# The two meta rows of w_out: scaled sums on VectorE in place of matmuls on TensorE, in a one-core hybrid decoder layer

## The chip, the core and the metric

The kernel runs on one core of a Trainium2 chip. A core has a matrix engine, TensorE (PE in the profile; PEld is its weight load), and three engines that work on 128 partitions: VectorE (DVE), ScalarE (ACT) and GpSimd (POOL). DMA transfers are started from queues; here nearly all loads and stores stand in the queue of SyncE (SP), one after the other. Each engine works through its own queue in the order in which the program was built, and waits by semaphore for what the others have to deliver.

The metric is the device time of one execution, in microseconds (us). Before the change it was 1255.82, the median of three runs (1255.19 to 1255.9).

## The reference, cut to what matters

One layer with 1024 tokens of width 1024, in front of which 16 meta tokens are put. Two branches, attention and a convolution, are merged by gates to `mixed`, which goes through `w_out`; the FFN behind it is convolved over three tokens.

```python
y_attn = a @ w_attn_proj
y_conv = c @ w_conv_proj
mixed = jax.nn.sigmoid(g_attn) * y_attn + jax.nn.sigmoid(g_conv) * y_conv
h = layer_norm(DEEPNORM_ALPHA * h + mixed @ w_out, ln1_g, ln1_b)
up = causal_dwconv(h @ ffn_w_up, ffn_dw, ffn_dw_b)
...
return h[:, N_META:]
```

The meta tokens' rows are dropped at the end. But the causal convolution with three taps reads two tokens back, so the last two meta rows of `h` behind `w_out` are needed for the first two real tokens. These two rows are what the change is about: `mixed[2 rows, 1024] @ w_out[1024, 1024]`, the residual and the norm.

## The kernel before

The kernel works in fp32. A product of two fp32 operands is made on TensorE from three matmuls in the type fp32r: each operand is split into a high part (a cast, line 267, on ScalarE) and a low part (the difference, line 270, on VectorE or GpSimd), and high x high, high x low and low x high are added in PSUM (`product`, lines 296, 300 and 301).

The stage of the projections (loop over `m` from line 1080) computes `mixed` in eight tiles of 128 channels. For each `m` it makes four groups of columns `g`, each with a product of the attention branch (PSUM tag `mm`, three buffers) and one of the convolution branch (tag `t`, two buffers). VectorE reads both from PSUM and multiplies by the gates (lines 1099 and 1100), adds (1101), ScalarE writes the high part (1108), and VectorE the low part (1109). In group 0 the first two columns are the two meta tokens; they go into the small tile `pair`, high parts in columns 0 and 1, low parts in 2 and 3 (lines 1103 and 1104).

`w_out` is loaded in eight blocks `k` of 128 rows. Blocks 0 to 3 go to free parts of the buffer FA ("early", line 1125, each placed in SP's queue behind the last gate load of tile m = k), blocks 4 and 5 to FA and OB, blocks 6 and 7 to the two rotating buffers `wr`. `prep_wo` splits them. The low parts of blocks 4 to 7 are formed on GpSimd.

The output stage (`out_rows`, line 1230) takes 128 tokens at a time, in the order 3, then -1 (the two meta rows), 7, 2, 6, 0, 4, 1, 5. For a tile it makes two halves of 512 columns, 24 matmuls each. VectorE evacuates a half and adds the residual (line 1253), collects its statistics (1254), aggregates them (241), ScalarE makes the root (246), and VectorE refines it (247 to 249) and normalises the row (1277). The next tile but one half, `turn` transposes it on TensorE (1287) and ScalarE writes the result (1300). For the two meta rows the kernel before uses 16 matmuls per half: for each block `k` one with the four columns of `pair` against the high part of `w_out` (line 1264), and one with the two high columns against the low part (1265). The sum has four partitions; ScalarE copies it (1266), and partitions 2 and 3 are brought to 0 and 1 by a DMA through SP (line 1271) so that VectorE can add them (1272).

The order on each engine is not that of the text. A scheduler places the instructions by priority (`rank`) and by its own estimate of when they are ready; `after` adds an edge of order. The built program is then fixed.

Of the kernel before, what the change touches and what calls it, by code (L numbers as in the profile page):

```python
# [23 lines left out]
F = mybir.dt.float32  # L24
R = mybir.dt.float32r
AF = mybir.ActivationFunctionType
OP = mybir.AluOpType
AX = mybir.AxisListType

P = 128  # L30
D = 1024
KC = D // P
# [31 lines left out]
RK_CLN, RK_OSPLIT, RK_Z, RK_CONV, RK_PROJ = 38000, 39000, 40000, 60000, 70000  # L64
# [35 lines left out]
def tile_hybrid_layer(  # L100
# [3 lines left out]
    nc = tc.nc  # L104
# [5 lines left out]
    def load(o, i):  # L110
        return nc.sync.dma_start(out=o, in_=i)
# [5 lines left out]
    def f32(ap):  # L117
        return ap.bitcast(F)

    def after(ins, first):  # L120

        tc.add_manual_dep(ins.ins, first.ins.name, mybir.DependencyInfo(
            mybir.DependencyClass.NoSync, mybir.DependencyReason.SCHED_ONLY), reason="order of work")

    @contextmanager
    def rank(p):

        saved = tc.cur_priority
        tc.cur_priority = p
        yield  # L130
        tc.cur_priority = saved


    const = ctx.enter_context(tc.tile_pool(name="const", bufs=1, side="left"))
# [6 lines left out]
    FA = arena.tile([P, 6144], F, name="FA")  # L141
# [23 lines left out]
    start = ExitStack()  # L165
# [100 lines left out]
    def split(raw, hi, lo, quick=False, behind=None):  # L266
        ins = nc.scalar.copy(hi, raw)  # L267
        if behind is not None:
            after(ins, behind)
        return (nc.vector if quick else nc.gpsimd).tensor_tensor(lo, raw, f32(hi), OP.subtract)  # L270
# [747 lines left out]
    for g in range(3):  # L1018
# [5 lines left out]
    rx_p = ctx.enter_context(tc.tile_pool(name="rx", bufs=1, side="right", reuse_waits="tile"))  # L1024
    RX = rx_p.tile([P, 2112], R, name="RX")
    wo_stack = ExitStack()
    RW = wo_stack.enter_context(tc.tile_pool(name="rw", bufs=1, side="right", reuse_waits="tile")).tile(
        [P, 2048], R, name="RW")
    RT = OB[:, 0:2048]


# [19 lines left out]
    def prep_wo(k, raw=None, behind=None):  # L1051
        if k < 4:
            hi, lo = OA[:, k * 2048:k * 2048 + 1024], OA[:, k * 2048 + 1024:k * 2048 + 2048]
        elif k < 6:
            hi, lo = ((RX, RW)[k - 4][:, x:x + 1024] for x in (0, 1024))
        else:
            hi, lo = (wsp_p.tile([P, D], R, name=n, tag=n) for n in ("whi", "wlo"))
        if raw is None:
            raw = wraw([P, D])
            load(raw, w_out_v[k])  # L1060
        split(raw, hi, lo, k < 4, behind)
        wo[k] = (hi, lo)

    pair = const.tile([P, KC, 4], R, name="pair")
    const.tile([P, 16], F, name="pad_e")
    g_next = [0]

    GS = [(FA, i * 516) for i in range(4)]
# [11 lines left out]
    for m in range(KC):  # L1080
        hi, lo = weights([P, KC, P], lambda raw: load(raw, w_ab[m]))

        def branch(i, g, tag, bufs):
            a, b = PG[g]
            ps = pat.tile([P, 512], F, name="ps_p", tag=tag, bufs=bufs)
            rhs = (oo, conv)[i]
            product(ps[:, :b - a], [(hi[:, 4 * i + k], lo[:, 4 * i + k], rhs(k, 0, a, b), rhs(k, 1, a, b))
                                    for k in range(4)])
            return ps[:, :b - a]

        def merge(g, psa, psb):
            a, b = PG[g]
            n = b - a
            with rank(RK_EVAC):
                t = gslot()[:, :, :n]
                ins = load(t, dram(sgd, m * P * U + a, [[U, P], [KC * P * U, 2], [1, n]]))

                ta, tb = t[:, 0], t[:, 1]
                nc.vector.scalar_tensor_tensor(ta, ta, 1.0, psa, OP.add, OP.mult)
                nc.vector.scalar_tensor_tensor(tb, tb, 1.0, psb, OP.add, OP.mult)  # L1100
                nc.vector.tensor_tensor(ta, ta, tb, OP.add)
                if g == 0:
                    nc.scalar.mul(pair[:, m, 0:2], ta[:, 0:2], 0.5)
                    nc.vector.scalar_tensor_tensor(pair[:, m, 2:4], ta[:, 0:2], 0.5, f32(pair[:, m, 0:2]),
                                                   OP.mult, OP.subtract)
                v = ta[:, n - 256:].rearrange("p (t x) -> p t x", t=2)
                h = mixed2(g, m, 0)
                last_act = nc.scalar.mul(h, v, 0.5)
                nc.vector.scalar_tensor_tensor(mixed2(g, m, 1), v, 0.5, f32(h), OP.mult, OP.subtract)
            return ins, last_act  # L1110

        if m < KC - 1:
            for g in range(4):
                last_gate, last_act = merge(g, branch(0, g, "mm", 3), branch(1, g, "t", 2))
        else:
            pa = [branch(0, g, "mm", 3) if g < 3 else branch(0, g, "s", 2) for g in range(4)]
            for g in range(4):
                last_gate, last_act = merge(g, pa[g], branch(1, g, "t", 2))
        if m in (2, 3):
            raw = (FA[:, 4112:5136], OB[:, 3072:4096])[m - 2]  # L1120
            load(raw, w_out_v[m + 2])
            prep_wo(m + 2, raw, last_act)
        if m < 4:
            early.append(FA[:, W_AT[m]:W_AT[m] + 1024])
            after(load(early[m], w_out_v[m]), last_gate)
    for k in range(4):
        prep_wo(k, early[k])
    prep_wo(6)
    prep_wo(7)

# [97 lines left out]
    def out_rows(i, between=(), work=()):  # L1230


        n, u = (P, 2 + i * P) if i >= 0 else (2, 0)
        if n == P:
            o = r_next[0] % 2 * 1024
            r_next[0] += 1
            whole = RT[:, o:o + 1024]
            load(whole, h0d[u:u + n, :])
        else:
            whole = OB[:, 3072:4096]  # L1240
        r = whole[:n]
        order = WO_ORDER if i != 5 else (0, 1, 2, 3, 6, 7, 4, 5)
        turned = None
        st = small.tile([P, 2, 6], F, name="st")
        pin = line if i in (0, 4, 1, 5) else lambda ins: ins
        for half in range(2):
            hs = slice(half * 512, half * 512 + 512)
            ps = pat.tile([P, 512], F, name="ps_w", tag="mm", bufs=3)
            if n == P:
                last = product(ps, [(mixed(i, k, 0), mixed(i, k, 1), wo[k][0][:, hs], wo[k][1][:, hs])  # L1250
                                    for k in order], turned)
                with rank(RK_TURN):
                    pin(nc.vector.tensor_tensor(r[:, hs], ps, r[:, hs], OP.add))
                    pin(nc.vector.bn_stats(st[:, half], r[:, hs]))
                turned = None
                if len(between) > half:
                    turned = turn(*between[half], behind=[last])
                if half == 0:
                    for f, *x in work:
                        f(*x)  # L1260
                continue

            for j, k in enumerate(order):
                nc.tensor.matmul(ps[:4], pair[:, k], wo[k][0][:, hs], start=j == 0, stop=False)
                last = nc.tensor.matmul(ps[:2], pair[:, k, 0:2], wo[k][1][:, hs], start=False, stop=j == KC - 1)
            nc.scalar.copy(whole[:4, hs], ps[:4])
        if n < P:
            q = FA[:4, 0:1024]
            load(q[0:2], h0d[0:2, :])
            nc.vector.tensor_tensor(r, r, q[0:2], OP.add)  # L1270
            load(q[0:2], whole[2:4])
            nc.vector.tensor_tensor(r, r, q[0:2], OP.add)
        with rank(RK_TURN):
            (mu, rs), = ln_stats([(r, n)], half_stats=st if n == P else None)
            for a in (512, 0) if i == 5 else (None,):
                x = r if a is None else r[:, a:a + 512]
                ins = pin(nc.vector.tensor_scalar(x, x, mu, rs, OP.subtract, OP.mult))
        if n == P:
            load(h1d[u - 2:u - 2 + P, :], r)
        return whole, n, ins  # L1280
# [93 lines left out]
    def edges():  # L1374
        with rank(RK_TURN):
# [7 lines left out]
            4: [(w_first, 2), (split_of, 1, BT2), (form_t4, 1)],  # L1383
            1: [(form_t3, 1), (w_first, 3)],
            5: [(form_t3, 0, EARLY), (form_t4, 0, EARLY)]}
    for i in (3, -1, 7, 2, 6, 0, 4, 1, 5):
        if i == -1:
            two = (i, *out_rows(i))
            continue
        rows = out_rows(i, ahead, work.get(i, ()))  # L1390
        ahead = [(i, *rows)]
        if i == 7:
            ahead.append(two)
        if i == 0:
            form_t2(1)
        if i == 4:
            split_of(1, BT4)
            split_of(1, BT1)
            edges()
        if i == 1:  # L1400
            split_of(1, BT3)
            split_of(0, B11, EARLY)
            split_of(0, B21, EARLY)
            form_t2(0, EARLY)
# [386 lines left out]
```

## Time and profile before

| what | value |
|---|---|
| runs | 1255.82 us median of three |
| profiled execution | 1255.65 us, its span 1253.9 us |
| TensorE clock granted in it | 0.999 of full speed |
| HBM | 150.29 MB read, 62.70 MB written |
| output stage, from 503 to 608 us of the span | 105 us, PE busy throughout |

The profile is one execution. Rows of its order of time give the start and the length in us, the engine, the line of the kernel, the operation and its operands (out<-in), a count, and in brackets the idle time of the engine before it and what ended that idle time. A busy engine is not necessarily one at its peak. The length of a matmul overlaps with that of the next one, so the distance of two starts is what a matmul costs; the same holds to a lesser degree for the other engines.

### The profile page before, as it was taken

The numbers are of one execution on the slowest core, as the hardware profiler recorded it, in microseconds if no ns is written. First come the engines' busy times: TensorE is split into PE (matmuls) and PEld (weight loads), VectorE is DVE, ScalarE is ACT, GpSimd is POOL, SyncE is SP. The second block draws the span as 40 slices with busy tenths as digits, with TensorE's granted clock in tenths as the row PEclk, the third lists the DMA queues.
The fourth block names the chain that finished last, engine by engine and source line by source line (L and its number), as shares of the span: only waits on it lengthen the run. The fifth ranks groups of instructions, "written<-read, shape, count | busy, mean of one in ns | idle before, by whom it ended". The sixth has DMA issues, their size and how long they took to land.

```text
span 1253.9 us, 21702 instructions
## 1 busy us (share of the span) xinstructions
PE 1241.6 (99%) x8546; PEld 1174.7 (94%) x8546; DVE 1081.1 (86%) x1876; ACT 586.7 (47%) x1056; POOL 12.3 (1%) x11
## 2 busy tenths in 40 slices
PE   9999999999999999999999999999999999999997
PEld 8999999999999999788899999999999998888886
DVE  7899989999978786648899999999999986996697
ACT  7522345645465233235565555554455553545330
POOL 0000000000000010000000000000000000000000
PEclk9999999999999999999999999999999999999999
DMA  7293733332255565222145565553464569988722
GB/s 280 71 312 103 183 107 95 109 93 87 68 147 142 182 173 139 77 75 101 68 135 187 192 210 189 186 215 120 167 218 167 204 207 318 387 317 315 251 85 84
DMA packets 96152, 212.10 MB, mean 169 GB/s; under 512 B 10787, under 2 KB 35939, under 8 KB 95922
## 3 DMA queue, kind: packets, MB, share of 16 engines
q1 hardware_dynamic: 84282, 199.64, 48.1%
q10 hardware_dynamic: 11768, 11.08, 2.7%
q8 instruction: 67, 1.10, 0.4%
q14 instruction: 35, 0.29, 0.1%
HBM read 150.29 MB, written 62.70 MB: 170 GB/s over the span
## 4 chain that ended last, share of the span: by engine, by line
PE 95%; DVE 3%; DMA 1%; issue 1%; ACT 0%; SPq 0%; DVEq 0%
PE px L1499 15%; PE py L1499 10%; PE ps_x L1637 9%; PE ps_z L1637 7%; PE ps_z L300 7%; PE ps_z L301 7%; PE ps_z L296 7%; PE pw L1499 5%; PE pz L1499 5%; PE ps_p L301 2%; PE ps_p L296 2%; PE ps_p L300 2%; PE ps_w L301 2%; PE ps_w L296 2%; PE ps_w L300 2%; PE ps_z L512 2%
## 5 line engine op out<-in xcount | busy, mean ns | idle before, releaser
L665 DVE SCALAR_TENSOR_TENSOR FA<-cin,cols,FA 128x1026 f32<-128x1026 f32 x120 | 152.5, 1280 | 0.3
L296 PE MATMUL ps_z<-RHO,whi 128*128 128x384 f32 (+2 forms) x324 | 104.2, 322 | 0.0
L300 PE MATMUL ps_z<-RHC,whi 128*128 128x384 f32 (+2 forms) x324 | 104.1, 321 | 0.0
L300 PE MATMUL ps_z<-RHO,whi 128*128 128x384 f32 (+2 forms) x324 | 104.0, 321 | 0.0
L301 PE MATMUL ps_z<-RHC,wlo 128*128 128x384 f32 (+2 forms) x324 | 103.8, 320 | 0.0
L296 PE MATMUL ps_z<-RHC,whi 128*128 128x384 f32 (+2 forms) x324 | 103.7, 320 | 0.0
L301 PE MATMUL ps_z<-RHO,wlo 128*128 128x384 f32 (+2 forms) x324 | 103.7, 320 | 0.0
L267 ACT CAST whi<-wr 128x1024 fp32r<-128x1024 f32 x37 | 39.0, 1053 | 69.1 <-PE ps_z L300 52.2
L1317 ACT CAST RHO<-wr 128x512 fp32r<-128x512 f32 x94 | 56.9, 621 | 24.2 <-DVE wr L1335 13.6
L1318 DVE TENSOR_TENSOR RHO<-wr,RHO 128x512 fp32r<-128x512 f32 x94 | 63.8, 690 | 4.5 <-ACT RHO L1317 4.2
L296 PEld LDWEIGHTS ps_z<-RHO,whi 128*128 128x128 f32 x324 | 61.0, 188 | 0.6 <-issue 0.3
L296 PEld LDWEIGHTS ps_z<-RHC,whi 128*128 128x128 f32 x324 | 61.1, 188 | 0.2
L301 PEld LDWEIGHTS ps_z<-RHO,wlo 128*128 128x128 f32 x324 | 61.0, 188 | 0.2
L301 PEld LDWEIGHTS ps_z<-RHC,wlo 128*128 128x128 f32 x324 | 60.9, 188 | 0.2
L1335 DVE TENSOR_TENSOR wr<-wr 128x512 f32<-128x512 f32 x88 | 61.0, 693 | 0.2
L300 PEld LDWEIGHTS ps_z<-RHO,whi 128*128 128x128 f32 x324 | 61.0, 188 | 0.1
L300 PEld LDWEIGHTS ps_z<-RHC,whi 128*128 128x128 f32 x324 | 60.9, 188 | 0.1
L672 ACT ACTIVATE FA<-ps_z,cols 128x384 f32<-128x384 f32 (+1 forms) x48 | 26.1, 543 | 50.3 <-PE ps_z L301 49.3
L1511 ACT COPY FA<-px 128x514 f32<-128x514 f32 (+2 forms) x23 | 13.2, 572 | 73.3 <-PE px L1499 73.3
L270 DVE TENSOR_TENSOR wlo<-wr,whi 128x1024 fp32r<-128x1024 f32 x35 | 42.6, 1218 | 4.8 <-ACT whi L267 4.1
L1318 DVE TENSOR_TENSOR ws<-wr,ws 128x512 fp32r<-128x512 f32 x60 | 40.9, 690 | 5.5 <-ACT ws L1317 5.3
L1424 ACT ACTIVATE FA<-OB,cols 128x512 f32<-128x512 f32 x44 | 36.0, 817 | 13.6 <-DVE OB L1507 13.6
(466 smaller groups left out, 3520.7 us busy)
## 6 DMA issues: line engine op xcount, KB each, us to landing
wr<-in_w_up_dram SPq DMA_DIRECT2D x44, 512.0 KB, 3.8
wr<-in_w_z_dram SPq DMA_DIRECT2D x30, 512.0 KB, 4.3
fd<-FA SPq DMA_DIRECT2D x44, 256.0 KB, 2.0
OB<-in_w_down_dram SPq DMA_DIRECT2D x19, 512.0 KB, 4.8
qt<-qd SPq DMA_DIRECT2D x28, 256.0 KB, 4.1
sgd<-FA ACTq DMA_DIRECT2D x32, 192.0 KB, 3.1
td<-OB SPq DMA_DIRECT2D x12, 512.0 KB
sums<-fd SPq DMA_DIRECT2D x12, 512.0 KB
```

Source lines behind the costliest of these rows:

```text
L267: ins = nc.scalar.copy(hi, raw)
L270: return (nc.vector if quick else nc.gpsimd).tensor_tensor(lo, raw, f32(hi), OP.subtract)
L296: ins = nc.tensor.matmul(ps, ah, bh, start=i == 0, stop=False)
L300: nc.tensor.matmul(ps, ah, bl, start=False, stop=False)
L301: last = nc.tensor.matmul(ps, al, bh, start=False, stop=i == n - 1)
L665: nc.vector.scalar_tensor_tensor(acc[c], cin[:, j:j + U], wc, acc[c], OP.mult, OP.add)
L1317: nc.scalar.copy(hi, src)
L1318: ins = nc.vector.tensor_tensor(lo, src, f32(hi), OP.subtract)
L1335: ins = nc.vector.tensor_tensor(*x)
L1424: nc.scalar.activation(t, cc[:, 2:HW], AF.Identity, bias=ffw(3, o), scale=ffw(2, o))
L1499: ins = nc.tensor.matmul(o, x[:, ks], bmat(sub, q, hl, k), start=first and k + j == 0, stop=k == 3 and j == 2, skip_group_check=not first)
L1637: nc.tensor.matmul(banks[i], l[:, ts], r[:, ws], start=first and a and x + k == 0, stop=z and x == len(ops) - 1 and k == 2, skip_group_che ...
```

## The change

The two meta rows are no longer a product of `pair` with the split `w_out`. Row t is a sum over the 1024 rows of `w_out`, each multiplied by one number. The new `two_rows(k)` adds block k, unsplit, to a running sum `two_sum[t]` of 128 partitions x 1024 columns: per partition the block's row times that partition's value in `pair`. For k = 0 these are two scaled copies on ScalarE, for the others two instructions on VectorE. After block 7 each sum is split into a high and a low part in the buffer OC (`two_parts`), and eight matmuls with the columns of a small tile `sel` of ones and zeros add up the 128 partitions of sum t into PSUM row t. `pair` is no longer split, four rows become two, and the transfer that brought partitions 2 and 3 to 0 and 1 is gone. The meta rows (-1) move from behind tile 3 to behind tile 2, between the third and the fourth tile of tokens, and the transposes of their result move with them. The calls: `two_rows(m - 2)` inside the loop over m, `two_rows(6)` behind it, `two_rows(7)` behind tile 3's normalisation, the two splits behind tile 7's.

```diff
-    RW = wo_stack.enter_context(tc.tile_pool(name="rw", bufs=1, side="right", reuse_waits="tile")).tile(
-        [P, 2048], R, name="RW")
+    wo_p = wo_stack.enter_context(tc.tile_pool(name="rw", bufs=1, side="right", reuse_waits="tile"))
+    RW = wo_p.tile([P, 2048], R, name="RW")
...
-    pair = const.tile([P, KC, 4], R, name="pair")
-    const.tile([P, 16], F, name="pad_e")
+    pair = const.tile([P, KC, 4], F, name="pair")
+    sel = const.tile([P, 16], R, name="sel")
+    nc.vector.memset(f32(sel), 0.0)
+    for t in range(2):
+        nc.vector.memset(f32(sel[:, 3 * t:3 * t + 1]), 1.0)
+    two_sum = [wo_p.tile([P, D], F, name=f"two{t}") for t in range(2)]
+    two_parts = [[OC[:, (2 * t + hl) * D:(2 * t + hl + 1) * D] for hl in range(2)] for t in range(2)]
+    wo_raw = {}
+
+    def two_rows(k, behind=None):
+
+        for t, a in enumerate(two_sum):
+            m = pair[:, k, t:t + 1]
+            if k == 0:
+                nc.scalar.activation(a, wo_raw[k], AF.Copy, scale=m)
+                continue
+            ins = nc.vector.scalar_tensor_tensor(a, wo_raw[k], m, a, OP.mult, OP.add)
+            if behind is not None:
+                after(ins, behind)
...
                     nc.scalar.mul(pair[:, m, 0:2], ta[:, 0:2], 0.5)
-                    nc.vector.scalar_tensor_tensor(pair[:, m, 2:4], ta[:, 0:2], 0.5, f32(pair[:, m, 0:2]),
-                                                   OP.mult, OP.subtract)
...
+        if m > 1:
+            with rank(RK_PROJ + 3000):
+                two_rows(m - 2)
     for k in range(4):
         prep_wo(k, early[k])
     prep_wo(6)
     prep_wo(7)
+    two_rows(6)
...
-            for j, k in enumerate(order):
-                nc.tensor.matmul(ps[:4], pair[:, k], wo[k][0][:, hs], start=j == 0, stop=False)
-                last = nc.tensor.matmul(ps[:2], pair[:, k, 0:2], wo[k][1][:, hs], start=False, stop=j == KC - 1)
-            nc.scalar.copy(whole[:4, hs], ps[:4])
+            for j in range(4):
+                nc.tensor.matmul(ps[:2], sel[:, j // 2 * 2:j // 2 * 2 + 2], two_parts[j // 2][j % 2][:, hs],
+                                 start=j == 0, stop=j == 3)
+            nc.scalar.copy(r[:, hs], ps[:2])
         if n < P:
-            q = FA[:4, 0:1024]
-            load(q[0:2], h0d[0:2, :])
-            nc.vector.tensor_tensor(r, r, q[0:2], OP.add)
-            load(q[0:2], whole[2:4])
-            nc.vector.tensor_tensor(r, r, q[0:2], OP.add)
+            q = FA[:2, 0:1024]
+            load(q, h0d[0:2, :])
+            nc.vector.tensor_tensor(r, r, q, OP.add)
...
-    for i in (3, -1, 7, 2, 6, 0, 4, 1, 5):
+    for i in (3, 7, 2, -1, 6, 0, 4, 1, 5):
...
+        if i == 3:
+            two_rows(7, rows[2])
         if i == 7:
+            for a, (hi, lo) in zip(two_sum, two_parts):
+                after(split(a, hi, lo, True), rows[2])
+        if i == 6:
             ahead.append(two)
```

More of the change, by code (lines that the diff above doesn't have):

```diff
@@ L1060, in prep_wo @@
             load(raw, w_out_v[k])
+        wo_raw[k] = raw
         split(raw, hi, lo, k < 4, behind)
         wo[k] = (hi, lo)
-    pair = const.tile([P, KC, 4], R, name="pair")
-    const.tile([P, 16], F, name="pad_e")
+    pair = const.tile([P, KC, 4], F, name="pair")
[15 more added lines that the diff above has]
+                after(ins, behind)
     g_next = [0]
@@ L1124, in tile_hybrid_layer @@
             early.append(FA[:, W_AT[m]:W_AT[m] + 1024])
+            wo_raw[m] = early[m]
             after(load(early[m], w_out_v[m]), last_gate)
+        if m > 1:
+            with rank(RK_PROJ + 3000):
+                two_rows(m - 2)
     for k in range(4):
```

## The prediction

> **What bounds the kernel now.** I read the page's totals first, then the chain that ended last.
>
> ```profile
> span 1253.9 us, 21702 instructions
> PE 1241.6 (99%) x8546; PEld 1174.7 (94%) x8546; DVE 1081.1 (86%) x1876; ACT 586.7 (47%) x1056; POOL 12.3 (1%) x11
> PE 95%; DVE 3%; DMA 1%; issue 1%; ACT 0%; SPq 0%; DVEq 0%
> ```
>
> TensorE (PE) carries 95% of the chain, so a matmul that goes is worth its place in PE's stream, unless PE then waits for something that the matmul used to cover. The next view is therefore the order of time on PE, from the first meta matmul to the transposes of tile 3.
>
> ```profile
> 515.48 0.40 PE L1264 MATMUL ps_w<-RX,pair 128*4 128x512 f32 x1
> 515.72 0.62 PE L296 MATMUL ps_w<-whi,RHC 128*128 128x512 f32 x2
> ...
> 524.06 0.40 PE L1265 MATMUL ps_w<-wlo,pair 128*2 128x512 f32 x1
> 524.29 0.39 PE L296 MATMUL ps_w<-RX,RHC 128*128 128x512 f32 x1
> ...
> 529.74 1.04 PE L1287 MATMUL ps_h<-cols,OB 128*128 128x128 f32 x8
> ```
>
> The reader is to see three things. The columns are start, duration, engine, line, operation. From 515.48 to 524.29 PE issues 38 matmuls, 32 of them for the meta rows and six that finish tile 3, one every 8.81 / 38 = 0.232 us: two weight columns cost what 128 cost. From 524.29 to 529.74 stand the 24 of tile 7's first half, 5.45 us, one every 0.227 us. And at 529.74 tile 3's transposes start at once. What they need is in VectorE's (DVE's) and ScalarE's (ACT's) rows of the same stretch:
>
> ```profile
> 518.93 1.29 DVE L1253 TENSOR_TENSOR OB<-ps_w,OB 128x512 f32<-128x512 f32 x2 [4.73 <-PE ps_w L301]
> 520.14 1.28 DVE L1254 BATCH_NORM_STATS2 st<-OB 128x6 f32<-128x512 f32 x2
> 521.45 0.21 DVE L241 BATCH_NORM_AGGREGATE mv<-st 128x2 f32<-128x12 f32 x1
> 523.64 0.81 DVE L1277 TENSOR_SCALAR OB<-OB,mv,sd 128x1024 f32<-128x1024 f32 x1
> 520.84 0.57 ACT L1266 COPY OB<-ps_w 4x512 f32<-4x512 f32 x1 [9.04 <-PE ps_w L1265]
> 521.43 1.28 ACT L246 ACT_TABLE_LOAD   x1
> ```
>
> Tile 3 is normalised at 523.64 + 0.81 = 524.45, and PE asks for it 5.3 us later. The meta matmuls are that cover.
>
> **The change part by part.** *Matmuls out and in.* 32 leave: 32 x 0.232 = 7.42 us. Eight come, of the same shape as those of line 1265 (two weight columns, 512 moved), between tile 2 and tile 6: 8 x 0.232 = 1.86. Nothing else on PE changes but places, so without a new wait the gain is 5.57 us.
>
> [...]
>
> *The new wait at tile 3's transposes.* Between 515.48 and the transposes stand 32 + 30 matmuls; without the 32, PE asks for tile 3 at 529.74 - 7.42 = 522.32. For DVE I need the delay from a matmul to its evacuation, and a chain not held by the table load:
>
> ```profile
> 541.30 0.39 PE L301 MATMUL ps_w<-whi,RHC 128*128 128x512 f32 x1
> 541.73 0.69 DVE L1253 TENSOR_TENSOR OB<-ps_w,OB 128x512 f32<-128x512 f32 x1 [2.02 <-PE ps_w L301]
> 542.46 0.69 DVE L1254 BATCH_NORM_STATS2 st<-OB 128x6 f32<-128x512 f32 x1
> 537.74 0.21 DVE L241 BATCH_NORM_AGGREGATE mv<-st 128x2 f32<-128x12 f32 x1
> 538.31 0.16 DVE L247 SCALAR_TENSOR_TENSOR sd<-mv,sd 128x1 f32<-128x1 f32 x1 [0.36 <-ACT sd L246]
> 538.90 0.81 DVE L1277 TENSOR_SCALAR OB<-OB,mv,sd 128x1024 f32<-128x1024 f32 x1
> ```
>
> An evacuation starts 0.43 after the start of the last matmul; line 247 starts 0.57 after line 241. The last matmul of tile 3's first half now has 13 ahead of it from 515.48: 515.48 + 13 x 0.227 = 518.43. So: evacuations at 518.86, statistics 1.21 later at 520.07, line 241 1.31 later at 521.38, line 247 at 521.95 (no copy of the meta sums stands ahead of the table load any more), line 248 at 522.15. Now the order of the built program decides. Between line 248 and line 249 of tile 3, DVE's queue has the evacuation of tile 7's first half. That half ends just where PE asks for the transposes: last matmul at 522.09, evacuation at 522.52. Behind it stand line 249, tile 7's statistics (0.73 after the evacuation, at 523.25) and tile 3's normalisation, 0.6 later (half of the 1.21 that two instructions in a row take) at 523.85 and 0.81 long: 524.66. PE waits 524.66 - 522.32 = 2.34 us. Bounds: 1.0 if the evacuation held nothing (normalised at 523.35), 3.4 if every step is as far off the other way. I take 2.3, since each step has its row.
>
> *Scaled sums during the projections.* Two per block k, k = 1 to 6, in the tiles m = 1 to 6; the nearest row is the depthwise convolution's, same operation and form. Those of k = 0 are two scaled copies on ACT, near a cast of that size.
>
> ```profile
> L665 DVE SCALAR_TENSOR_TENSOR FA<-cin,cols,FA 128x1026 f32<-128x1026 f32 x120 | 152.5, 1280 | 0.3
> L267 ACT CAST whi<-wr 128x1024 fp32r<-128x1024 f32 x37 | 39.0, 1053 | 69.1 <-PE ps_z L300 52.2
> 451.10:462.20 11.10, 11.10 (x99) 11.10 (x98) 9.65 (x19) 3.73 (x8) 2.44 (x1) 1.00 0.69 191
> 462.20:473.50 11.30, 11.30 (x97) 11.30 (x97) 9.55 (x18) 3.63 (x8) 2.39 (x1) 1.00 0.55 142
> 473.50:484.60 11.10, 11.10 (x99) 11.10 (x98) 7.63 (x18) 2.78 (x7) 0.00 (x0) 1.00 0.54 142
> 452.47 2.44 POOL L270 TENSOR_TENSOR RX<-FA,RX 128x1024 fp32r<-128x1024 f32 x1 [449.15 <-ACT RX L267]
> 452.55 2.65 DVE L1109 SCALAR_TENSOR_TENSOR RHC<-OB,RHC 128x256 fp32r<-128x256 f32 x1
> 467.88 0.41 DVE L1100 SCALAR_TENSOR_TENSOR OB<-OB,ps_p 128x256 f32<-128x256 f32 x1
> 478.14 0.42 DVE L1100 SCALAR_TENSOR_TENSOR OB<-OB,ps_p 128x256 f32<-128x256 f32 x1 [0.53 <-PE ps_p L301]
> 480.86 0.42 DVE L1100 SCALAR_TENSOR_TENSOR OB<-OB,ps_p 128x256 f32<-128x256 f32 x1 [0.60 <-PE ps_p L301]
> ```
>
> The window rows give stretch, length, then busy time of PE, PEld, DVE, ACT, POOL. A tile takes PE 11.1 us, and DVE 7.63 of them. Two sums of 1.28 make 10.2, which fits. In tiles m = 3 and 4 GpSimd's (POOL's) difference holds one DVE instruction for 2.65 us where its like take 0.42, DVE stands at 9.65, and 12.2 no longer fits: each runs 1.0 late. Queued behind the sums are the reads that free PSUM. A conv-branch product has two banks; two products take 480.86 - 478.14 = 2.72, so one takes 1.36 and its bank is wanted again three products, 4.1 us, after its end. The worst is m = 4, g = 1: read at 467.88 in the trace, 2.6 us later behind the sums and some 0.3 more behind POOL, done at 471.2. Its product ends a tile (11.2) before 478.14, at 466.9, so PE wants the bank at 471.0, and at 471.8 as built, since seven matmuls of the next tile (1.36 / 12 = 0.11 us each) now stand ahead. I take 0 us; the bounds are 0 and 1.5 for the two tiles.
>
> ACT's copies for k = 0 (2 x 1.05) fit the gap before 422.88, when ACT next has work. Block 2 is the raw block that comes latest:
>
> ```profile
> 422.88 0.42 ACT L1108 ACTIVATE RHC<-FA 128x256 fp32r<-128x256 f32 x1 [2.31 <-DVE FA L1101]
> 438.52 0.46 SPq L111 DMA_DIRECT2D FA<-in_w_out_dram  x1
> DMA to landing us min/median/max: 3.5/4.1/4.6
> 442.99 0.42 DVE L1099 SCALAR_TENSOR_TENSOR OB<-OB,ps_p 128x256 f32<-128x256 f32 x1 [0.53 <-PE ps_p L301]
> ```
>
> It lands by 438.52 + 4.6 = 443.1, and DVE comes to its sums after 442.99 + 0.33: no wait, at most some tenths.
>
> *After tile 3.* The sums of k = 7 (2.6 us) follow tile 3's normalisation, 524.7 to 527.2; tile 7's second half ends near 531. The splits (two casts of 1.05 on ACT, two differences of about 1.2 on DVE) end near 537, and the eight matmuls come near 543. The load of w_up rows that waits for block 7's buffer moves from before tile 3's store to behind it, some 12 us; the first read of any such rows is the last row of the next fence, 50 us on. All cost 0.
>
> *The meta rows behind tile 2.* DVE's queue now has their residual (1.21 us, as its row below) and statistics ahead of tile 2's normalisation. Counted from tile 2's last matmul: the copy of the second meta half ends at 1.86 + 0.43 + 0.57 = 2.9, the residual at 4.1, two statistics and five short steps at about 6.0, the normalisation at 6.8. PE asks for it after the eight matmuls and half a tile: 0.23 + 1.86 + 5.45 = 7.5. The cover is 0.7 us; I take 0. One residual (1.21) and a read-back over DRAM, whose landing DVE awaited for 2.06 us, are gone; PE never waited for them.
>
> ```profile
> 525.15 1.21 DVE L1270 TENSOR_TENSOR OB<-OB,FA 2x1024 f32<-2x1024 f32 x1 [0.70 <-ACT OB L1266]
> 528.43 1.21 DVE L1272 TENSOR_TENSOR OB<-OB,FA 2x1024 f32<-2x1024 f32 x1 [2.06 <-DMA FA<-OB]
> 614.19 0.97 PE L1499 MATMUL pw<-RHC,RHO 128*128 128x256 f32 x6 [0.98 <-ACT FA L1300]
> 579.66 1.28 DVE L1318 TENSOR_TENSOR RHO<-wr,RHO 128x512 fp32r<-128x512 f32 x2
> ```
>
> **Sum.** -7.42 + 1.86 + 2.34 = -3.2 us. The profiled execution took 1255.65 us (span 1253.9 and 1.75 around it), 0.17 below the median of 1255.82. Forecast: 1255.65 - 3.2 = 1252.4 us.
>
> **The rivals.** (1) *VectorE holds PSUM a little:* the 0.6 us of margin in m = 4 (and less in m = 3) fails, or tile 2's cover of 0.7. That is 0.5 to 2 us: 1253.0 to 1254.5. For it: 12.2 us of work in 11.1. Against it: the seven matmuls moved ahead.
> (2) *No lasting wait at tile 3:* the wait is 1 us or less, 1250.1 to 1251.1. Against it: the evacuation stands in the queue.
> (3) *VectorE becomes the bound of the projections:* over six tiles it is asked for 4 x 7.63 + 2 x 9.6 + 12c against 6 x 11.2, with 2.7 of tolerance. That is 49.6 + 12c against 69.9: covered at c = 1.28, late from c = 1.7 on, and all gain gone at 1.95, which is the point from which it decides. At the 2.65 us of the instruction that POOL held, DVE is 11.5 us late: 1264. Against it: 120 rows at 1.28. For it: sums that read two SBUF operands, as the held one did.
> (4) *PE's clock drops in the pause.* The longest pause of the trace's later part is the 0.98 us above, with the matmuls after it at full rate; 2.3 us isn't shown. If the next half tile (5.5 us) ran at half rate, the loss is 5.5: 1258. [...]
>
> **How the numbers follow.** The forecast 0.56, rival 1 0.22, rival 2 0.08, rival 3 0.08, rival 4 0.06. The range holds the forecast with the wait's bounds, rivals 1 and 2: 1250.0 to 1255.0. A change of 0.2% is 2.5 us, about what can be told from none, so 1253.3 is the edge: the forecast is beyond it in most of its spread, rival 2 fully, rival 1 mostly not. Faster 0.59, within 0.28, slower 0.13.
>
> **What would show it.** Right: no more than eight meta matmuls at about 0.23 us; PE idle 2 to 2.7 us ahead of tile 3's transposes, released by DVE's normalisation, with the evacuation of tile 7 ahead of it; no PE idle among the ps_p products; scaled sums of 1.28; transposes of tile 2 without a wait. Wrong: waits of PE on DVE's line-1119 reads in m = 3 and 4; sums near 2 us; matmuls of twice the length after the pause.

## The result, and the profile after

The changed kernel takes 1254.04 us, the median of 22 runs (1252.69 to 1256.36). The kernel before took 1255.84 us in runs between them, the median of 22 (1254.71 to 1256.91). The ratio is 0.9986, with a 95% interval of 0.9979 to 0.9992: 1.8 us faster where 3.2 were forecast. The profiled execution took 1253.91 us. The page's first lines and the shares of its chain:

```profile
span 1252.1 us, 21686 instructions
PE 1237.1 (99%) x8522; PEld 1173.4 (94%) x8522; DVE 1093.1 (87%) x1886; ACT 589.9 (47%) x1060; POOL 12.7 (1%) x11
PE 94%; DVE 2%; DMA 2%; issue 1%; ACT 0%; SPq 0%; DVEq 0%; ACTq 0%
```

TensorE has 24 matmuls less (8522 against 8546), VectorE 12 us more, and TensorE still sets the end. Where the time went is best read stage by stage, between three starts on TensorE: the first matmul of the projections, the first of the output stage, the first of the stage behind it. The order of time of the kernel before has them in these rows:

```profile
416.04 0.28 PE L296 MATMUL ps_p<-OA,whi 128*128 128x258 f32 x1
...
503.12 0.39 PE L296 MATMUL ps_w<-RX,RHC 128*128 128x512 f32 x1
...
607.76 0.40 PE L1499 MATMUL px<-OC,RHO 128*128 128x256 f32 x2
```

and that of the changed kernel in these:

```profile
416.66 0.28 PE L296 MATMUL ps_p<-OA,whi 128*128 128x258 f32 x1
...
504.18 0.39 PE L296 MATMUL ps_w<-RX,RHC 128*128 128x512 f32 x1
...
605.71 0.28 PE L1524 MATMUL px<-OC,RHO 128*128 128x256 f32 x1
```

| stage, us | before | after | difference |
|---|---|---|---|
| up to the projections | 416.04 | 416.66 | +0.62 |
| projections | 87.08 | 87.52 | +0.44 |
| output stage | 104.64 | 101.53 | -3.11 |
| from there to the end of the span | 646.14 | 646.39 | +0.25 |
| span | 1253.9 | 1252.1 | -1.8 |

The output stage, about which the prediction's sum was made, gained 3.11 us against the forecast 3.2. The other three rows are the difference. Of them only the projections' 0.44 us will turn out to belong to the change. (These are figures of one execution each; in the change's the granted clock is 1.00 from 522 to 530 us, around the pause.) The profile shows one thing less: the spread of the runs, 3.7 us against 2.2 before.

In the output stage the order of time shows the forecast pause as it was drawn (columns as before; a bracket gives the idle time ahead and what ended it):

```profile
519.94 1.29 DVE L1275 TENSOR_TENSOR OB<-ps_w,OB 128x512 f32<-128x512 f32 x2 [4.66 <-PE ps_w L301]
...
522.46 0.21 DVE L241 BATCH_NORM_AGGREGATE mv<-st 128x2 f32<-128x12 f32 x1
...
523.14 0.39 PE L301 MATMUL ps_w<-whi,RHC 128*128 128x512 f32 x1
523.22 0.16 DVE L248 SCALAR_TENSOR_TENSOR sd<-sd 128x1 f32<-128x1 f32 x1
523.57 0.69 DVE L1275 TENSOR_TENSOR OB<-ps_w,OB 128x512 f32<-128x512 f32 x1 [0.19 <-PE ps_w L301]
524.17 0.15 DVE L249 SCALAR_TENSOR_TENSOR sd<-sd 128x1 f32<-128x1 f32 x1
524.29 0.69 DVE L1276 BATCH_NORM_STATS2 st<-OB 128x6 f32<-128x512 f32 x1
524.90 0.80 DVE L1297 TENSOR_SCALAR OB<-OB,mv,sd 128x1024 f32<-128x1024 f32 x1
...
525.75 1.09 PE L1307 MATMUL ps_h<-cols,OB 128*128 128x128 f32 x8 [2.23 <-DVE OB L1297]
...
526.60 0.47 PE L296 MATMUL ps_w<-RX,RHC 128*128 128x512 f32 x1
```

TensorE ends tile 7's first half at 523.14 + 0.39 and stands for 2.23 us. Between lines 248 and 249 of tile 3 VectorE evacuates tile 7's half, and its statistics stand ahead of tile 3's normalisation too.

### The profile page after: what moved, and what is told of

It is laid out like the page before. It is cut to its first block, busy times and chain, and to the rows that moved or that the text cites. A ratio compares the mean times of both kernels' runs of the same rounds, so it can differ in the third digit from the quotient of the medians.

```text
span 1252.1 us, 21686 instructions
## 1 busy us (share of the span) xinstructions
PE 1237.1 (99%) x8522; PEld 1173.4 (94%) x8522; DVE 1093.1 (87%) x1886; ACT 589.9 (47%) x1060; POOL 12.7 (1%) x11
## 4 chain that ended last, share of the span: by engine, by line
PE 94%; DVE 2%; DMA 2%; issue 1%; ACT 0%; SPq 0%; DVEq 0%; ACTq 0%
PE px L1524 15%; PE py L1524 9%; PE ps_x L1662 9%; PE ps_z L300 7%; PE ps_z L1662 7%; PE ps_z L301 7%; PE ps_z L296 7%; PE pz L1524 5%; PE pw L1524 5%; PE ps_p L296 2%; PE ps_p L301 2%; PE ps_p L300 2%; PE ps_w L301 2%; PE ps_w L296 2%; PE ps_w L300 2%; PE ps_z L512 2%
## 5 line engine op out<-in xcount | busy, mean ns | idle before, releaser
L1524 PE MATMUL px<-OA,RHO 128*128 128x258 f32 (+1 forms) x324 | 42.2, 279 | 0.0
```

The lines of the kernel that those rows point to most:

```text
L1524: ins = nc.tensor.matmul(o, x[:, ks], bmat(sub, q, hl, k), start=first and k + j == 0, stop=k == 3 and j == 2, skip_group_check=not first)
```

## The experiments

Eleven kernels were run, each beside runs of the kernel before. Times are medians in us; the ratio to the kernel before has its 95% interval; the last columns are the stages of the profiled execution, read as above.

| kernel | time (lowest to highest, runs) | before | ratio | projections | output stage |
|---|---|---|---|---|---|
| the change | 1254.04 (1252.69 to 1256.36, 22) | 1255.84 | 0.9986 [0.9979, 0.9992] | 87.52 | 101.53 |
| e1_norm_first | 1251.15 (1251.05 to 1251.64, 5) | 1255.26 | 0.9968 [0.9955, 0.998] | 87.52 | 100.26 |
| e2_turn_later | 1250.43 (1249.84 to 1251.21, 5) | 1255.26 | 0.9962 [0.9949, 0.9974] | 87.52 | 99.10 |
| e3_no_sums | 1253.63 (1251.41 to 1254.0, 11) | 1255.26 | 0.9984 [0.9975, 0.9993] | 87.08 | 101.51 |
| e4_sums_twice | 1261.57 (1261.06 to 1261.96, 4) | 1255.17 | 1.0049 [1.0035, 1.0062] | 90.66 | 107.34 |
| e5_long_pause | 1257.18 (1256.34 to 1257.86, 11) | 1255.17 | 1.0015 [1.0006, 1.0024] | 87.51 | 106.44 |
| e6_move_only | 1258.45 (1256.95 to 1259.4, 8) | 1255.17 | 1.0023 [1.0012, 1.0034] | 87.08 | 108.57 |
| e7_old_place | 1254.46 (1252.08 to 1255.83, 11) | 1255.26 | 0.999 [0.9981, 0.9999] | 87.51 | 104.11 |
| e8_later_pinned | 1249.95 (1249.48 to 1250.76, 5) | 1255.19 | 0.9959 [0.9947, 0.9972] | 87.75 | 99.08 |
| e9_fill_matmuls | 1254.92 (1254.62 to 1255.3, 10) | 1255.19 | 0.9998 [0.9989, 1.0007] | 87.51 | 103.87 |
| e10_fill_transposes | 1255.53 (1254.77 to 1256.53, 10) | 1255.19 | 1.0002 [0.9993, 1.0011] | 87.51 | 103.90 |
| e11_change_filled | 1252.79 (1251.96 to 1253.04, 11) | 1255.19 | 0.998 [0.9971, 0.9989] | 87.51 | 101.54 |

The two stages repeat to 0.01 us between kernels that have the same code there, so they can be read to a tenth. The time up to the projections does not: over all these profiles it lies between 414.89 and 416.66 us, by how long TensorE waits for the first loads (0 to 1.3 us) and for a tile of the attention (0 to 0.9 us). The +0.62 of the first table is inside that spread, and so is not put down to the change. The time behind the output stage lies between 646.1 and 647.0 us in all of them, so its +0.25 is not either.

### The pause at tile 3

Two kernels treat the pause in two ways. The first orders one instruction of VectorE:

```diff
-                    pin(nc.vector.tensor_tensor(r[:, hs], ps, r[:, hs], OP.add))
+                    ins = pin(nc.vector.tensor_tensor(r[:, hs], ps, r[:, hs], OP.add))
+                    if i == 7 and half == 0:
+                        after(ins, between[0][3])
```

Here `between[0][3]` is tile 3's normalisation.

> The evacuation of tile 7's first half is ordered behind tile 3's normalisation on VectorE; nothing else is asked for. Theory (the 2.23 us pause ahead of tile 3's transposes is in part that evacuation and the statistics queued with it): the pause falls to 1.0 us, the time to 1254.0 - 1.2 = 1252.8 us. Rival (the evacuation holds nothing, the chain from tile 3's last matmul is that long by itself): pause 2.2 us, 1254.0 us.

```profile
522.27 0.81 DVE L1299 TENSOR_SCALAR OB<-OB,mv,sd 128x1024 f32<-128x1024 f32 x1
522.99 0.68 DVE L1275 TENSOR_TENSOR OB<-ps_w,OB 128x512 f32<-128x512 f32 x1
...
523.13 1.09 PE L1309 MATMUL ps_h<-cols,OB 128*128 128x128 f32 x8 [0.95 <-DVE OB L1299]
```

In the order of time of e1_norm_first the normalisation comes first and TensorE stands for 0.95 us. The output stage took 101.53 - 100.26 = 1.27 us less, as the theory has it. But the time fell by more: 4.1 us below its own before, where the change is 1.8 below. Something else went with the pause.

The second kernel gives the transposes another half tile of cover:

```diff
-                if len(between) > half:
+                if len(between) > half and between[half]:
...
+        if i == 7:
+            ahead = [None] + ahead
         rows = out_rows(i, ahead, work.get(i, ()))
```

> Tile 3's transposes go behind tile 7's second half instead of its first; nothing else is moved. Theory (the pause is the cover that the meta matmuls gave, and half a tile, 5.5 us, covers it as well): no pause of TensorE there, 1254.0 - 2.2 = 1251.8 us. Rival (the pause only comes back later, since ScalarE's and VectorE's work behind the transposes is wanted in time): a new wait of 1 to 2 us between 530 and 615, 1253 to 1254 us.

In its order of time the transposes follow a matmul without a gap (the view ends within them, so the row counts six of the eight):

```profile
529.63 0.40 PE L301 MATMUL ps_w<-RW,RHC 128*128 128x512 f32 x1
529.87 0.82 PE L1307 MATMUL ps_h<-cols,OB 128*128 128x128 f32 x6
```

The output stage is at 104.64 - 99.10 = 5.54 us below the kernel before. That is the 5.57 us which 24 matmuls less were worked out to give. No wait came back between 530 and 615. The time, 1250.4 us, is again further down than 2.2 us below the change.

The next kernel takes the kernel before and moves its old meta rows alone:

```diff
-    for i in (3, -1, 7, 2, 6, 0, 4, 1, 5):
+    for i in (3, 7, 2, -1, 6, 0, 4, 1, 5):
...
-        if i == 7:
+        if i == 6:
             ahead.append(two)
```

> The kernel before with one thing changed: its meta rows (all 32 matmuls of the old scheme) stand between the third and the fourth token tile, as in the change. Theory (the pause comes from the place alone): TensorE waits 2.2 us ahead of tile 3's transposes, nothing else changes, 1255.8 + 2.2 = 1258.0 us. Rival (the pause comes from VectorE's new sums or splits): no pause, 1255.8 us.

The pause appears with no sum or split in the program: it comes from the place alone. But the output stage lost 108.57 - 104.64 = 3.93 us with a pause of 2.23. The order of time around it, and then the busy time by stretches (stretch, length, busy PE, PEld, DVE, ACT, POOL, then the clock granted to TensorE, DMA share and GB/s):

```profile
521.81 0.39 PE L301 MATMUL ps_w<-whi,RHC 128*128 128x512 f32 x1
524.43 1.97 PE L1287 MATMUL ps_h<-cols,OB 128*128 128x128 f32 x8 [2.23 <-DVE OB L1277]
526.05 0.78 PE L296 MATMUL ps_w<-RX,RHC 128*128 128x512 f32 x1
526.62 0.63 PE L300 MATMUL ps_w<-RX,RHC 128*128 128x512 f32 x1
527.05 0.63 PE L301 MATMUL ps_w<-RX,RHC 128*128 128x512 f32 x1
```

```profile
522.00:524.00 2.00, 0.20 (x1) 0.00 (x0) 1.82 (x5) 0.00 (x0) 0.00 (x0) 1.00 0.00 0
524.00:526.00 2.00, 1.57 (x8) 1.57 (x9) 0.37 (x1) 0.36 (x2) 0.00 (x0) 0.55 0.42 160
526.00:528.00 2.00, 2.00 (x7) 1.64 (x6) 0.00 (x0) 2.00 (x7) 0.00 (x0) 0.59 0.27 104
528.00:530.00 2.00, 2.00 (x10) 1.65 (x9) 0.00 (x0) 0.54 (x2) 0.00 (x0) 1.00 0.02 6
```

Behind the pause the clock is at half (0.55 and 0.59 as the means of the two stretches there; e5_long_pause, below, has three whole stretches at 0.50): eight transposes take 1.62 us in place of 0.85, and matmuls stand 0.43 us apart in place of 0.227. From the two rows, (0.45 + 0.41) x 2 us / 0.5 = 3.4 us at half clock, and 3.93 - 2.23 = 1.7 us lost by it. The same pause in the profiled execution of the change was followed by matmuls at 0.227 and a granted clock of 1.00. The eight runs of e6_move_only fall into two groups, four from 1257.0 to 1257.8 us and four from 1259.1 to 1259.4, whose medians are again 1.7 us apart.

### The clock

The runs of a kernel list the mean granted clock of each execution, which shows something of this without a trace: 3.4 us at half clock are 0.0014 of 1254 us. Of the 22 runs of the change, 11 show 0.998 or 0.999, with a median of 1253.2 us (1252.69 to 1253.91), and 11 show 0.997, with a median of 1254.7 us (1254.16 to 1256.36). No run of e1_norm_first or e2_turn_later is under 0.998. The listed figure is not sharp: two of the four longer runs of e6_move_only list 0.998, and one run of the kernel before, 1257.27 us long, lists 0.997, for which there is no trace. The change has no trace of an execution at 0.997 either, so what happens in these is inferred from e6_move_only, and tested below by filling the pause. To make the loss sure, the next kernel lengthens the pause by putting block 7's sums ahead of the normalisation (`root[0]` is line 249's instruction):

```diff
+            held = two_rows(7, root[0]) if i == 3 else ()
             for a in (512, 0) if i == 5 else (None,):
...
                 ins = pin(nc.vector.tensor_scalar(x, x, mu, rs, OP.subtract, OP.mult))
+                for first in held:
+                    after(ins, first)
...
-        if i == 3:
-            two_rows(7, rows[2])
```

> The two sums of block 7 are put between tile 3's root and its normalisation on VectorE, so that TensorE's pause ahead of the transposes grows by 2.47 us to 4.7 us. Theory (a pause costs its own length): 1254.0 + 2.5 = 1256.5 us, transposes and the following matmuls at their old distance of 0.13 and 0.227 us. Rival (the clock falls in a pause of this length and the matmuls after it take twice as long for some us): distance 0.45 us for 3 us or more, 1258 us or more.

```profile
524.00:526.00 2.00, 0.00 (x0) 0.00 (x0) 2.00 (x3) 1.20 (x2) 0.00 (x0) 0.97 0.00 0
526.00:528.00 2.00, 0.82 (x4) 0.82 (x5) 1.13 (x2) 0.89 (x1) 0.00 (x0) 0.50 0.49 176
528.00:530.00 2.00, 2.00 (x9) 1.81 (x8) 0.00 (x0) 1.60 (x5) 0.00 (x0) 0.50 0.87 338
530.00:532.00 2.00, 2.00 (x7) 1.52 (x6) 0.00 (x0) 1.29 (x4) 0.00 (x0) 0.50 0.05 18
532.00:534.00 2.00, 2.00 (x9) 1.65 (x8) 0.00 (x0) 0.00 (x0) 0.00 (x0) 0.83 0.36 104
```

The stretches of e5_long_pause show the half clock for (0.03 + 1.5 + 0.17) x 2 / 0.5 = 6.8 us, twice as long as in e6_move_only, and all 11 of its runs are at 0.996 or 0.997. The time, 1257.2, is between what the two theories gave. The stage tells them apart: 106.44 - 99.10 = 7.34 us over the kernel without a pause, 4.56 of them the pause. The other 2.8 fit the clock: it falls at 525.9 by these stretches and the transposes start at 527.18, so 1.3 of the 6.8 us lie in the pause and cost nothing, and the 5.5 behind it lose half of their length.

Two kernels then fill that pause, once with matmuls and once with transposes, results unused:

```diff
+                    if i == 7 and half == 0:
+                        pd = pat.tile([P, 512], F, name="ps_e", tag="t", bufs=2)
+                        with rank(RK_TURN):
+                            for _ in range(18):
+                                ins = nc.tensor.matmul(pd, mixed(7, 4, 0), wo[4][0][:, hs], start=True, stop=True)
+                                after(ins, last)
+                                last = ins
                     turned = turn(*between[half], behind=[last])
```

In the other kernel the loop has 40 turns of `nc.tensor.transpose(pd[:, 0:P], ident, ident)`.

> The kernel with the pause of 4.6 us, filled with 18 idle matmuls of 0.227 us (4.1 us, result unused). Theory (the clock falls because TensorE stands still): transposes and matmuls behind the pause at 0.10 and 0.227 us, time 1257.2 - 2.5 = 1254.7 us. Rival (the loss is that of the late normalisation, not of the clock): 1257.2 us.

> The kernel with the pause of 4.6 us, filled with 40 idle transposes of 0.10 us (4.0 us, result unused) in place of matmuls. If transposes hold the clock as matmuls do: 1254.7 us, distances of 0.10 and 0.227 us behind them. [...]

The order of time of e10_fill_transposes:

```profile
522.55 4.53 PE L1288 MATMUL ps_e<-cols 128*128 128x128 f32 x40
527.27 1.09 PE L1322 MATMUL ps_h<-cols,OB 128*128 128x128 f32 x8 [0.19 <-DVE OB L1310]
528.12 0.48 PE L298 MATMUL ps_w<-RX,RHC 128*128 128x512 f32 x1
528.44 0.40 PE L302 MATMUL ps_w<-RX,RHC 128*128 128x512 f32 x1
528.67 0.40 PE L303 MATMUL ps_w<-RX,RHC 128*128 128x512 f32 x1
```

With matmuls the output stage falls from 106.44 to 103.87 us, with transposes to 103.90, although the normalisation is as late as before. No run of either kernel is under 0.998. (The profiled execution with transposes is longer than the one with matmuls by 0.8 us behind 607 us, where the two kernels are the same; so the 0.6 us between their medians is not read as a cost of the transposes.) So the loss is the clock's, and the clock falls because TensorE stands still: with the pause open all 11 runs list 0.996 or 0.997, with it filled none of 20 is under 0.998. Transposes held it here as matmuls did.

The last kernel of this group fills the pause of the change itself, with nine such matmuls in the same place.

> The changed kernel with nine idle matmuls (2.04 us, result unused) in TensorE's queue between tile 7's first half and tile 3's transposes, where the 2.23 us pause stands. Theory (in about half of the executions the granted clock falls behind this pause, which costs 1.5 us, and it falls because TensorE stands still): no execution at a granted clock of 0.997 or less, median 1253.2 us, highest under 1254.2. Rival (the spread has another source): median 1254.0 us, highest over 1255, half of the executions at 0.997.

All 11 runs are at 0.998 or 0.999 and end by 1253.04; the spread is 1.1 us where the change has 3.7. The profiled stage is that of the change, 101.54. Nine useless matmuls make the kernel 2.4 us faster than before in the median, where without them it is 1.8.

### The scaled sums in the projections

> Leaves out the scaled sums of blocks 1 to 6 (12 VectorE instructions in the projections), so the two meta rows hold blocks 0 and 7 alone. Theory (the sums lie beside TensorE's work and cost nothing): 1254.0 us, within 0.3. Rival (VectorE holds the projections up a little): first matmul of the output stage 0.3 to 0.5 us earlier against the start of the projections, 1253.5 us; if VectorE is the bound, 1250 us or less.

The edit takes `two_rows(m - 2)` for m > 2 and `two_rows(6)` out. The projections return to 87.08 us, exactly those of the kernel before, and the output stage stays. The sums thus cost 0.44 us, directly or through the order of matmuls: without them the scheduler gives TensorE the order of the kernel before again. The time agrees where the listed clock is 0.998: the five such runs have a median of 1252.2, 3.0 us below their before, where the change's 11 are 2.6 below theirs (one of the five, at 1254.0, is as long as those at 0.997). TensorE shows no idle time among these matmuls; what differs is their distance. In tile m = 3, one product of twelve matmuls from its first to the first of the next, in the kernel before:

```profile
455.50 0.28 PE L296 MATMUL ps_p<-OA,whi 128*128 128x256 f32 x1
...
456.86 0.28 PE L296 MATMUL ps_p<-OC,whi 128*128 128x256 f32 x1
```

and in the changed kernel:

```profile
456.18 0.28 PE L296 MATMUL ps_p<-OA,whi 128*128 128x256 f32 x1
...
457.60 0.28 PE L296 MATMUL ps_p<-OC,whi 128*128 128x256 f32 x1
```

1.36 us against 1.42, so 0.113 and 0.118 us a matmul. Both distances occur in both kernels, for whole tiles. In the kernel before the odd tiles run at the short one, in the changed kernel, whose order of matmuls at the seams of the tiles is another, tiles 1 and 4. Whether the order or VectorE's work is the cause was tried on the best kernel so far, by tying TensorE to the old order:

```diff
-            product(ps[:, :b - a], [(hi[:, 4 * i + k], lo[:, 4 * i + k], rhs(k, 0, a, b), rhs(k, 1, a, b))
-                                    for k in range(4)])
+            last = product(ps[:, :b - a], [(hi[:, 4 * i + k], lo[:, 4 * i + k], rhs(k, 0, a, b), rhs(k, 1, a, b))
+                                           for k in range(4)], made[-1] if m < KC - 1 or g * i == 0 else None)
+            made.append(last)
```

> On the kernel with tile 3's transposes half a tile later: TensorE's order in the projections is tied to that of the kernel before (no first product of the next tile ahead of the last of this one), the scaled sums stay. Theory (the 0.44 us that the projections take longer, 87.52 against 87.08 us, come from TensorE's new order of matmuls alone): 87.1 us, 1250.4 - 0.4 = 1250.0 us. Rival (the sums hold the PSUM buffers, and the new order covered it, as the prediction's third step has it): TensorE waits 0.3 to 2 us for the reads of line 1119 in m = 3 and 4, 1250.7 to 1252.4 us.

```profile
459.43 0.28 PE L301 MATMUL ps_p<-OA,wlo 128*128 128x256 f32 x1
459.93 0.38 PE L296 MATMUL ps_p<-OC,whi 128*128 128x256 f32 x1 [0.23 <-DVE OB L1121]
```

Both were at work. The short distance came back in the odd tiles, so it goes with the order. But the stage is longer, 87.75 us: at 459.43 a matmul is followed half a microsecond later by the next, which waited for VectorE's read of a PSUM buffer, behind the sums of m = 3. A smaller delay (0.18 us between two matmuls, at 448.13) stands behind those of m = 2. With the new order the sums cost 0.44 us in matmul distance, with the old one 0.67 in waits. The time, 1249.95, cannot be told from that of e2_turn_later, and the hit on the forecast's number is chance: its stage went the other way.

The third rival's price was tried by issuing each sum twice (a second `two_rows(m - 2)` for m > 2, a second `two_rows(6)`).

> Every scaled sum of blocks 1 to 6 is issued twice (12 more VectorE instructions of 1.25 us in the projections), so these blocks count double in the two meta rows. By the sum of the third rival, 49.6 + 12 x 2.5 = 79.6 us of VectorE against 66.9 + 2.7: about 10 us late, 1264 us. If the margins are wider than was worked out: under 1257 us. If VectorE held TensorE up already with one sum each: over 1266 us.

The projections took 3.1 us more than with single sums, not 10, with three waits of TensorE for reads of line 1119, 4.0 us together, in the tiles m = 4 and 5. The rest of VectorE's backlog went out of the stage and came back as a pause of 5.0 us at tile 3, 2.8 more than in the change. The output stage is 107.34 - 101.53 = 5.8 us longer; the half clock behind the pause (3.4 us, from 531.8 on) is part of the remaining 3.0, which were not followed further. Behind the three waits in the projections, of 1.32, 1.64 and 1.01 us, the granted clock stays at 1.00 in this execution. So a backlog of VectorE costs TensorE less than was worked out, and much of it later.

### The new scheme in the old place

This kernel puts `two_rows(7)` and the two splits right behind `two_rows(6)`, goes back to the order 3, -1, 7, and ties the meta rows' residual behind tile 3's normalisation.

> The new scheme in the old place: sums of block 7 and the two splits go into the last tile of the projections, the eight meta matmuls between tile 3 and tile 7, and the meta rows' residual behind tile 3's normalisation. Theory (the pause comes from the missing cover: eight matmuls give 1.86 us of it back, and no evacuation stands ahead of the normalisation): pause 0 to 0.4 us, 1251.8 to 1252.2 us. Rival (sums and splits ahead of tile 3's evacuation delay it as much as the cover gives): pause 2 us, 1254 us.

```profile
516.43 0.89 SPq L111 DMA_DIRECT2D OB<-h0d  x2
...
521.95 1.29 DVE L1278 TENSOR_TENSOR OB<-ps_w,OB 128x512 f32<-128x512 f32 x2 [4.97 <-DMA OB<-h0d]
...
522.70 0.50 PE L296 MATMUL ps_w<-RX,RHC 128*128 128x512 f32 x1 [3.13 <-DVE OB L1278]
```

Neither theory had this. With the sums and splits in the last tile VectorE reads the last gates out of OB later; the transfer that brings tile 3's residual into OB is issued at 516.43 (511.05 in the change), and lands at 521.95. VectorE waits for it, and TensorE for a PSUM buffer, 3.13 us, again with the half clock behind (seven matmuls at 0.427 us, 3.4 us of half clock). Seven of the 11 runs are at 0.997.

## Why the prediction came out as it did

**Matmuls out and in: right.** 24 fewer, 5.57 us worked out, 5.54 measured where no pause interferes (e2_turn_later). The eight new ones, from the first to the next matmul behind them, took 545.81 - 543.95 = 1.86 us:

```profile
543.95 2.02 PE L1286 MATMUL ps_w<-OC,sel 128*2 128x512 f32 x8
545.81 0.39 PE L296 MATMUL ps_w<-RX,RHC 128*128 128x512 f32 x1
...
549.49 0.81 DVE L1297 TENSOR_SCALAR OB<-OB,mv,sd 128x1024 f32<-128x1024 f32 x1
...
551.29 0.60 PE L1307 MATMUL ps_h<-cols,OB 128*128 128x128 f32 x4
```

**The meta rows behind tile 2: right.** The last two rows are tile 2's normalisation and its transposes. The normalisation ends at 550.30, 6.6 us after tile 2's last matmul at 543.73 (6.8 forecast), and TensorE asks at 551.29, 7.6 after it (7.5 forecast).

**The pause: right in size and mechanism.** 2.34 forecast, 2.23 shown as idle time, by the queue order that was named. The forecast counted from the moment at which the next matmul could have started, 523.14 + 0.23 = 523.37; so counted the pause is 525.75 - 523.37 = 2.38, and the stages of the change and of e2_turn_later differ by 101.53 - 99.10 = 2.43. The bound of 1.0 without the evacuation is the 0.95 of e1_norm_first. It comes from the place of the meta rows, not from the new work (e6_move_only).

**What a pause costs: the step that failed.** The forecast charged the pause with its own length, and its fourth rival gave the clock's fall a chance of 0.06 and a price of 5.5 us. In half of the change's runs the clock falls behind the pause, by their listed clock, at 1.5 us (1254.7 against 1253.2), and 1.7 in e6_move_only. The rival had the cause; its price was over three times too high, and its chance too low. That the whole next half tile runs at half rate was the author's assumption: the runs showed 3.4 us of half clock behind the pause of 2.23 us (e6_move_only), and 6.8 with one of 4.56 (e5_long_pause). So the median stands between two kinds of execution, and filling the pause leaves the one with the full clock alone (e11_change_filled, 11 of 11 runs at 0.998 or 0.999). A pause of 2.23 us was enough in half of the change's runs, one of 0.95 in none of the five of e1_norm_first. Why the same pause is followed by the half clock in one execution and not in the next, no run here shows.

**Scaled sums in the projections: in the bounds, not at the value taken.** Taken 0, bounds 0 to 1.5, measured 0.44. Each sum took 1.28 us as forecast (the group of line 1081; columns are count, then lowest, median and highest duration in ns, first and last start, and shape), and GpSimd's difference held one addition in each of m = 3 and 4 (2.20 and 2.18 us where their like take 0.42; GpSimd's own ran from 453.78 for 2.57 us and from 465.24 for 2.59):

```profile
L1081 DVE SCALAR_TENSOR_TENSOR two<-FA,pair,two x8: 1276/1279/1285, 432.8 to 469.6; 128x1024 f32<-128x1024 f32 x8
...
445.55 2.48 DVE L1081 SCALAR_TENSOR_TENSOR two<-FA,pair,two 128x1024 f32<-128x1024 f32 x2 [1.51 <-DMA FA<-in_w_out_dram]
454.43 2.20 DVE L1120 TENSOR_TENSOR OB<-OB 128x258 f32<-128x258 f32 x1
```

The margin was argued with the seven matmuls moved ahead. They did cover: in the old order TensorE waits (e8_later_pinned), in the new it doesn't. What was missed is that the new order has a price of its own. (The third rival's 4 x 7.63 + 2 x 9.6 is 49.7, not 49.6, which changes nothing.) The second row is the load of block 2: "no wait, at most some tenths" was 1.51 us, since it landed some 6.4 us after its issue (439.14) where 4.6 was the largest shown before; in the change no wait of TensorE follows from it.

**The rivals.** The first, VectorE holding PSUM a little (1253.0 to 1254.5), has the time right by chance: 0.44 us are lost there, though not as a wait, and what brings the median from 1253.2 to 1254.0 is the clock. The second, no lasting wait, is refuted by the 2.23. The third, VectorE as the bound, needs doubled sums to show even 3.1 us inside the projections. The fourth is what happens in half of the executions, at 1.5 us and not at its 5.5. In the rest the forecast -3.2 + 0.44 = -2.8 us is to be compared with the 2.6 us that the change's 11 runs at 0.998 or 0.999 are below their before. A gain of 1.8 us is clear of noise by its interval, but it is less than the 2.5 us that the forecast took as its edge: what came is "within", to which it gave 0.28, and not "faster" at 0.59.

**Beyond the change.** Tile 3's transposes half a tile later bring the whole 5.5 us: e2_turn_later is 4.8 us faster than the kernel before (ratio 0.9962), 3.0 more than the change.

## What to carry to other kernels

Work that is taken off the bounding engine is worth its time only if nothing used it as cover: look for the next thing that the engine asks for, and move that too. Price a pause of TensorE like those here at its length and what the clock lost behind it (1.7 us behind 2.23 in the profiled execution of e6_move_only, 2.8 behind 4.56 in that of e5_long_pause), unless the executions show that the clock stays up; if the pause can't be closed, idle matmuls in it can be cheaper than none, as nine were here (1252.79 us against 1254.04). Look at the granted clock of every run, not at that of the profiled one alone: a median may lie between two kinds of execution.

## What the runs showed of the hardware

- Behind a pause of TensorE the granted clock fell to about half: to 0.55 and 0.59 as means of two stretches of 2 us in the profiled execution of e6_move_only (2.23 us), to 0.50 through three such stretches in that of e5_long_pause (4.56 us). It did so behind 2.23 us in about half of the executions (11 of 22 by the listed clock in the change, four of eight by time in e6_move_only), behind 3.13 us in seven of 11 (e7_old_place, listed 0.997), behind 4.56 us in all 11 (listed 0.996 or 0.997), behind 0.95 us in none of five (e1_norm_first, listed 0.998 or 0.999), and not behind pauses of 1.01 to 1.64 us in the profiled execution of e4_sums_twice (1.00 from 417 to 505 us). It stayed there for 3.4 us in the profiled executions of e6_move_only, e7_old_place and e4_sums_twice, and for 6.8 us in that of e5_long_pause; the length did not follow that of the pause, since e4_sums_twice has the longest, 5.04 us. Pauses between 1.64 and 2.23 us were not tried.
- Forty transposes of 128x128 in fp32, 0.113 us each, held the clock through 4.5 us as 18 matmuls did: none of the 10 runs of either kernel lists less than 0.998. The matmuls before them stood 0.227 us apart, so the clock was at full; other types, and transposes behind a lower clock, were not tried.
- Matmuls of 256 columns stand 0.113 or 0.118 us apart, for whole tiles, with no idle time shown. It goes with the order of the matmuls at the seams of the tiles (e3_no_sums and e8_later_pinned have the order of the kernel before, and its short odd tiles), and repeats between kernels of the same order. What sets it stays open.
